# A hybrid retention and SSD block: first loads in smaller pieces, meta-token products padded to 128 rows, the last row block's end in another order

## The chip, the cores and the metric

The kernel runs on one core of a Trainium2 chip. The metric is the device time of one execution in microseconds. The core has a matrix engine (TensorE, PE in the profile; its weight loads are listed as PEld), a vector engine (DVE), a scalar engine (ACT), a general engine (POOL), and the sync engine (SP), which here only issues transfers. ACT issues some transfers too. The engines run side by side and wait for each other through semaphores; each of them does its own instructions in order.

## What is computed

One layer of a hybrid encoder over 512 frames of width 1024, behind 16 learned meta tokens. Cut to what matters:

```
hn = rmsnorm(h) * norm1_w
q, k, v, g, z, xbc, dt = split(hn @ w_in)           # 1024 x 7184
y_ret = GroupNorm(retention(q, k, v)) * silu(g)     # 8 heads of 128
y_ssd = GatedRMSNorm(ssd(silu(conv4(xbc)), dt), z)  # 4 groups of 4 heads of 64
h = h + concat(y_ret, y_ssd) @ w_out                # 2048 x 1024
h = h + relu(rmsnorm(h) @ w_ff1)**2 @ w_ff2         # 1024 x 4096 x 1024
out = rmsnorm(h)[the 512 frames] * final_norm_w
```

Retention and SSD both carry a state from one run of tokens to the next. The meta tokens form a first, short run of 16; its contribution to the first state is a product over 16 tokens for each SSD group and for each retention head. All values are float32. Each large product is done as three: both operands are split into a part that the matrix engine's fast float32 format (fp32r) holds and the rest, and high by high, high by rest and rest by high are summed.

## The kernel before

**Start (lines 128 to 315).** Twenty products of zeros (`warm`, L135) run on PE while the first transfers are under way. The transposed input comes as `xr` in two runs of tokens, 272 and 256, each in two transfers of four of the eight slices of width 128 (L147, on SP's queue, behind `pc`, the column constants with norm1's weights). The first weights `wzr` (the z columns of SSD group 0 and the dt columns) come in two transfers on ACT's queue (L143). Then SP issues the meta tokens, row constants, two of the four row blocks of x, the identity, the two weight transfers of the next projection (`ahead_load(1)`), the other two row blocks, and `cst`. `gain_split` (L273, L274) makes the high part `hnh` of a slice on DVE or ACT and the rest `hnl` on DVE; `split` (L151, L152) does the same for weights, ACT the high part and DVE the rest. `inv_rms` (L280 to L282) takes each row block's sum of squares on ACT and its power on POOL.

**First projection.** `z_first` (L420) multiplies two pairs of 128-token blocks; the second pair needs the second run of tokens. A small product for the meta tokens' dt (`pdm`, L427) needs `hm` (L424) from DVE. Then `conv_silu` runs the B columns of group 0: a product over 272 tokens, then `rms_row` as a hook (L289 to L294: small PE products that turn the row factors into a row `rsr`), then the eviction of the first product with `rsr` (L393), then a product over 256 tokens and its eviction. Four columns of convolution on DVE (L397, L399) follow.

**Weaving.** The SSD cores and the retention cores are generators, advanced by one step each time the projection in front yields, so their small float32 products lie between the projection's. `dt_gen` computes the step sizes on DVE (L338 to L353) and then the cumulative sums on PE (`acs`, L359). The tile framework orders the instructions of each engine by program order and by its own estimate of when they are ready.

**Meta-token products.** In `ssd_core` the first state is a product of `bt[:M, 3, :]` and `xmw`, both 16 rows high (L528), once for each of 4 groups. In `ret_core` it is `mk[:, 0, :]` by `mk[:, 1, :]`, 16 rows high (L685), once for each of 8 heads. A plain float32 product shows as two records on PE.

**End.** `token_gemm` multiplies by w2 for two halves of 512 columns; in each, the last four (or two) k-slices are finished block by block, so that block 3's products end last (L779). `fin_b`, for each of four blocks of 128 rows, adds the product to the residual (DVE, L1026), sums squares (ACT, L1041), forms the factor (POOL, L1042, L1043), scales the second half (DVE, L1044) and the first half (ACT, L1046) and writes them from SP's and ACT's queues (L1045, L1047). `nwb` holds the final norm's weights on all rows (loaded at L1061).

## Time and profile before

| | |
|---|---|
| median of 3 runs | 866.22 us (866.08 to 866.31) |
| the profiled execution | 866.04 us |
| its span, first to last instruction | 864.3 us |
| PE busy | 851.9 us (99%) |
| DVE, ACT, POOL busy | 557.8, 406.6, 30.9 us |
| moved | 84.69 MB, mean 98 GB/s |

In the profile PE's clock is the granted one, as a share of full speed. A row of the timeline gives the start, the duration, the engine, the line, the operation, the written and the read names, the shapes, a count of merged instructions, and, in brackets, how long the engine had been idle before and what ended that.

### The profile page before, as it was taken

Reading aid. Unit: us, or ns where it says so; the run is one execution under the profiler, and the core shown is the slowest. Engines: PE = TensorE matmul, PEld = TensorE weight load, DVE = VectorE, ACT = ScalarE, POOL = GpSimd, SP = SyncE. Lnnn points to the kernel's source line nnn. Section 1 sums busy time; section 2 is a strip of 40 time slices with the busy share of each in tenths; the row PEclk is TensorE's granted clock in tenths of the full one; section 3 lists DMA queues with packets and bytes.
Section 4 is the critical chain, followed back from the end, with each engine's and each line's share of the span. In section 5 each row is a group of like instructions: output and inputs, shape, how many; then the busy total and the mean of one; then the engine's idle time right before and its main releaser. Section 6 shows DMA issues by size and latency. Waiting matters only on the chain.

```text
span 864.3 us, 13343 instructions
## 1 busy us (share of the span) xinstructions
PE 851.9 (99%) x5566; PEld 767.4 (89%) x5566; DVE 557.8 (65%) x872; ACT 406.6 (47%) x683; POOL 30.9 (4%) x58
## 2 busy tenths in 40 slices
PE   8999999999999999999999999999999999999995
PEld 6999999999889988999888889999999888888884
DVE  5799887978745564455455549988887544464432
ACT  6673627272432323232353457577667533443432
POOL 1000010010000000000000000000000000000001
PEclk9999999999999999999999999999999999999999
DMA  8833323333231313122222221333335433332002
GB/s 314 241 124 98 114 85 97 113 84 98 74 98 49 98 50 98 55 93 58 89 84 91 86 66 65 99 98 99 98 99 164 153 98 98 97 98 98 0 1 98
DMA packets 84221, 84.69 MB, mean 98 GB/s; under 512 B 2336, under 2 KB 67104, under 8 KB 84160
## 3 DMA queue, kind: packets, MB, share of 16 engines
q1 hardware_dynamic: 83296, 81.68, 30.7%
q10 hardware_dynamic: 864, 2.16, 0.7%
q8 instruction: 43, 0.70, 0.3%
q14 instruction: 18, 0.15, 0.1%
HBM read 81.70 MB, written 2.13 MB: 97 GB/s over the span
## 4 chain that ended last, share of the span: by engine, by line
PE 91%; DVE 5%; ACT 1%; issue 1%; DMA 1%; POOL 1%; POOLq 0%; SPq 0%; DVEq 0%; ACTq 0%
PE acc L753 10%; PE acc L754 10%; PE acc L752 10%; PE fb L970 8%; PE fd L970 5%; PE pj L324 3%; PE pj L326 3%; PE pj L325 3%; PE fa L970 3%; PE pz L447 3%; PE pk L324 2%; PE pk L326 2%; PE pv L324 2%; PE pv L326 2%; PE pv L325 2%; PE pk L325 2%
## 5 line engine op out<-in xcount | busy, mean ns | idle before, releaser
L151 ACT ACTIVATE wh<-wr 128x1024 fp32r<-128x1024 f32 x146 | 153.8, 1057 | 215.5 <-issue 66.8
L152 DVE TENSOR_TENSOR wh<-wr,wh 128x1024 fp32r<-128x1024 f32 x146 | 178.1, 1222 | 116.9 <-ACT wh L151 116.8
L753 PE MATMUL acc<-wh,mh 128*128 128x512 f32 x370 | 145.7, 394 | 0.4 <-DVE mh L152 0.4
L752 PE MATMUL acc<-wh,mh 128*128 128x512 f32 x370 | 145.9, 396 | 0.0
L754 PE MATMUL acc<-wh,mh 128*128 128x512 f32 x370 | 145.7, 394 | 0.0
L753 PEld LDWEIGHTS acc<-wh,mh 128*128 128x128 f32 x370 | 69.4, 188 | 17.0 <-DVE mh L152 0.9
L754 PEld LDWEIGHTS acc<-wh,mh 128*128 128x128 f32 x370 | 69.4, 188 | 16.4
L752 PEld LDWEIGHTS acc<-wh,mh 128*128 128x128 f32 x370 | 69.3, 188 | 15.8
L324 PE MATMUL pj<-hnh,wh 128*128 128x256 f32 (+2 forms) x256 | 73.7, 288 | 0.0
L326 PE MATMUL pj<-hnh,wh 128*128 128x256 f32 (+2 forms) x256 | 72.8, 285 | 0.0
L325 PE MATMUL pj<-hnl,wh 128*128 128x256 f32 (+2 forms) x256 | 72.8, 284 | 0.0
L970 PE MATMUL fb<-hs,wh 128*128 128x256 f32 x576 | 70.7, 280 | 0.1
L970 PEld LDWEIGHTS fb<-hs,wh 128*128 128x128 f32 x576 | 69.1, 188 | 0.3 <-DVE wh L152 0.3
L325 PEld LDWEIGHTS pj<-hnl,wh 128*128 128x128 f32 x256 | 48.4, 189 | 0.0
L324 PEld LDWEIGHTS pj<-hnh,wh 128*128 128x128 f32 x256 | 48.3, 189 | 0.0
L326 PEld LDWEIGHTS pj<-hnh,wh 128*128 128x128 f32 x256 | 48.2, 188 | 0.0
L970 PE MATMUL fa<-hs,wh 128*128 128x256 f32 x384 | 47.8, 281 | 0.3 <-ACT a_lo L975 0.3
L970 PE MATMUL fd<-hs,wh 128*128 128x256 f32 x384 | 46.7, 280 | 0.0
L970 PEld LDWEIGHTS fa<-hs,wh 128*128 128x128 f32 x384 | 46.1, 189 | 0.4 <-ACT a_lo L975 0.4
L970 PEld LDWEIGHTS fd<-hs,wh 128*128 128x128 f32 x384 | 45.9, 188 | 0.1
L151 ACT ACTIVATE mh<-a_lo 128x512 fp32r<-128x512 f32 x48 | 29.4, 623 | 20.6 <-PE acc L754 18.3
L152 DVE TENSOR_TENSOR mh<-a_lo,mh 128x512 fp32r<-128x512 f32 x48 | 32.5, 687 | 8.9 <-ACT mh L151 8.9
(265 smaller groups left out, 1651.7 us busy)
## 6 DMA issues: line engine op xcount, KB each, us to landing
wr<-in_w_ff_dram SPq DMA_DIRECT2D x30, 1024.0 KB, 5.3
wr<-in_w_in_dram SPq DMA_DIRECT2D x40, 512.0 KB, 5.2
wr<-in_w_out_dram SPq DMA_DIRECT2D x8, 1024.0 KB, 5.0
wr<-in_w_in_dram SPq DMA_DIRECT2D x7, 1024.0 KB, 8.6
lt<-acsd SPq DMA_DIRECT2D x16, 256.0 KB, 3.9
xt<-in_x_dram SPq DMA_DIRECT2D x4, 512.0 KB, 9.0
a_lo<-in_w_ff_dram SPq DMA_DIRECT2D x2, 1024.0 KB, 6.8
wzr<-in_wzd_dram ACTq DMA_DIRECT2D x2, 544.0 KB, 5.4
```

The lines of the kernel that those rows point to most:

```text
L151: ACT.activation(dst_h, src, AF.Copy)
L152: DVE.tensor_tensor(dst_l, src, dst_h.bitcast(F32), op=ALU.subtract)
L324: PE.matmul(ps[:, :n], lhsT=wh[:, k, :], rhs=hnh[:, k, t0:t0 + n], start=(k == 0), stop=False)
L325: PE.matmul(ps[:, :n], lhsT=wh[:, k, :], rhs=hnl[:, k, t0:t0 + n], start=False, stop=False)
L326: PE.matmul(ps[:, :n], lhsT=wl[:, k, :], rhs=hnh[:, k, t0:t0 + n], start=False, stop=(k == KT - 1))
L447: PE.matmul(o, lhsT=a[:, k, tk], rhs=zp[k // 4][y][:, k % 4, :], start=(i == 0), stop=(i == len(seq) - 1))
L752: PE.matmul(acc[b], lhsT=s[:, 0, tk], rhs=wh[:, kk, :], start=(k == 0), stop=False)
L753: PE.matmul(acc[b], lhsT=s[:, 1, tk], rhs=wh[:, kk, :], start=False, stop=False)
L754: PE.matmul(acc[b], lhsT=s[:, 0, tk], rhs=wl[:, kk, :], start=False, stop=(k == nk - 1))
L970: PE.matmul(o, lhsT=w[:, y, k, cs], rhs=h[:, z, k, :], start=(q in (1, 6, 5) and t == 0 and k == 0 and i == 0), stop=(k == 3 and i == 2), ...
```

## The change

Fewer products of zeros run at the start (13 for 20). `pc` moves from SP's queue to the head of ACT's; `wzr` comes in three transfers (slices 0 and 1, 2 and 3, 4 to 7) and the first run of `xr` likewise, the second run still in two; the first weight half is split in two pieces. The two transfers of the next projection's weights go ahead of the meta tokens and x. In the one `conv_silu` with a hook, both products come first, then `rms_row`, then both evictions. The meta-token operands become buffers of 128 rows that POOL fills with zeros once (`btm`, `xmw`, and two `mk`), of which 16 rows are written, and their products take all 128 rows. At the end, block b's sum and squares come ahead of the scaling of block b-1; the last block is summed and scaled in runs of 256 columns; the weights `nwb` are scaled by the square root of 1024 on ACT, so that the mean's division goes. The diff, cut to its core (the layout of `wzd` follows that of `wzr`):

```diff
-NWARM = 20
+NWARM = 13
...
+    btm = sp.tile([P, P], F32, name="btm")
+    xmw = sp.tile([P, 256], F32, name="xmw")
     POOL.memset(ones, 1.0)
...
-    nc.sync.dma_start(out=pc, in_=pcols)
-    for j in range(2):
-        nc.scalar.dma_start(out=wzr[:, j], in_=wzd[:, j])
-    for i, (t0, n) in enumerate(HV):
-        for j in range(2):
-            o = KT * t0 + 4 * j * n
-            nc.sync.dma_start(out=xr[i][:, 4 * j:4 * j + 4, :], in_=xtr[:, o:o + 4 * n].rearrange("p (k n) -> p k n", n=n))
+    nc.scalar.dma_start(out=pc, in_=pcols)
+    for k0, k1 in ((0, 2), (2, 4), (4, 8)):
+        nc.scalar.dma_start(out=wzr[:, k0:k1], in_=wzd[:, k0:k1])
+    for i, k0, k1 in ((0, 0, 2), (0, 2, 4), (0, 4, 8), (1, 0, 4), (1, 4, 8)):
+        t0, n = HV[i]
+        o = KT * t0 + k0 * n
+        nc.sync.dma_start(out=xr[i][:, k0:k1, :], in_=xtr[:, o:o + (k1 - k0) * n].rearrange("p (k n) -> p k n", n=n))
...
-            split(hv, lv, wzr[:, j])
+            for k0, k1 in ((0, 2), (2, 4)) if j == 0 else ((0, 4),):
+                split(hv[:, k0:k1], lv[:, k0:k1], wzr[:, 4 * j + k0:4 * j + k1])
...
+    ahead_load(1)
     nc.sync.dma_start(out=mt, in_=meta)
     nc.sync.dma_start(out=hr, in_=hrows.partition_broadcast(P))
-    for b in range(2):
+    for b in range(NB):
         nc.sync.dma_start(out=xt[b], in_=x[b * P:(b + 1) * P, :])
-    nc.sync.dma_start(out=idt, in_=cident)
-    ahead_load(1)
-    for b in range(2, NB):
-        nc.sync.dma_start(out=xt[b], in_=x[b * P:(b + 1) * P, :])
+        if b == 1:
+            nc.sync.dma_start(out=idt, in_=cident)
     POOL.memset(dtv, 0.0)
+    POOL.memset(btm, 0.0)
+    POOL.memset(xmw, 0.0)
     nc.sync.dma_start(out=cst, in_=cpack)
...
+        def evict(ps, t0, n):
+            DVE.tensor_tensor(pre[:, 3 + t0:3 + t0 + n], ps[:, :n], rsr[:, t0:t0 + n], op=ALU.mult)
+        out = []
         for t0, n in ((t_in, 272 - t_in), (272, 256)):
             ps = psum(pp, "pj")
             mm_cols(ps, n, wh, wl, t0)
-            if hook:
-                hook()
-                hook = None
-            DVE.tensor_tensor(pre[:, 3 + t0:3 + t0 + n], ps[:, :n], rsr[:, t0:t0 + n], op=ALU.mult)
+            out.append((ps, t0, n))
+            if not hook:
+                evict(*out.pop())
+        if hook:
+            hook()
+            for o in out:
+                evict(*o)
...
-        xmw = sw.tile([M, 256], F32, tag="xmw", name="xmw", bufs=1)
-        bt = sw.tile([P, 4, P], F32, tag="bt", name="bt", bufs=1)
+        bt = sw.tile([P, 3, P], F32, tag="bt", name="bt", bufs=1)
...
-        ACT.activation(bt[:M, 3, :], psm[:M, 256:256 + P], AF.Copy)
+        ACT.activation(btm[:M], psm[:M, 256:256 + P], AF.Copy)
...
-        PE.matmul(ps[:, :256], lhsT=bt[:M, 3, :], rhs=xmw, start=True, stop=True)
+        PE.matmul(ps[:, :256], lhsT=btm, rhs=xmw, start=True, stop=True)
...
-        mk = rw.tile([M, 2, P], F32, tag="mk", name="mk")
+        mk = RC["mk"][h % 2]
...
-        DVE.tensor_scalar(mk[:, 0, :], psm[:M, 0:P], cst[:M, K_KDM + h:K_KDM + h + 1], None, op0=ALU.mult)
-        ACT.activation(mk[:, 1, :], psm[:M, P:2 * P], AF.Copy, scale=rsc[:M, 0:1])
+        DVE.tensor_scalar(mk[:M, 0, :], psm[:M, 0:P], cst[:M, K_KDM + h:K_KDM + h + 1], None, op0=ALU.mult)
+        ACT.activation(mk[:M, 1, :], psm[:M, P:2 * P], AF.Copy, scale=rsc[:M, 0:1])
...
+            RC["mk"] = [rp.tile([P, 2, P], F32, name=f"mk{i}") for i in range(2)]
+            for t in RC["mk"]:
+                POOL.memset(t, 0.0)
...
-        add_h2(0)(b, acc)
-        ss = small.tile([P, 1], F32, tag="ss", name="ss")
-        ACT.activation(yo[b][:, H0], xt[b][:, H0], AF.Square, accum_out=ss)
-        POOL.tensor_scalar(ep[b], ss, 1.0 / D, EPS, op0=ALU.mult, op1=ALU.add)
-        DVE.tensor_tensor(yo[b][:, H0], xt[b][:, H0], nwb[:, H0], op=ALU.mult)
+        v = xt[b][:, H0]
+        DVE.scalar_tensor_tensor(v, acc, rs2[b], v, op0=ALU.mult, op1=ALU.add)
+        ACT.activation(yo[b][:, H0], v, AF.Square, accum_out=ep[b])
+        POOL.tensor_scalar(ep[b], ep[b], D * EPS, None, op0=ALU.add)
+        DVE.tensor_tensor(yo[b][:, H0], v, nwb[:, H0], op=ALU.mult)
     def fin_b(b, acc):
-        add_h2(1)(b, acc)
-        ss = small.tile([P, 1], F32, tag="ss", name="ss")
-        rs = small.tile([P, 1], F32, tag="rs", name="rs")
-        ACT.activation(yo[b][:, H1], xt[b][:, H1], AF.Square, accum_out=ss)
-        POOL.tensor_scalar(rs, ss, 1.0 / D, ep[b], op0=ALU.mult, op1=ALU.add)
+        last = b == NB - 1
+        for c in (slice(512, 768), slice(768, 1024)) if last else (H1,):
+            v = xt[b][:, c]
+            DVE.scalar_tensor_tensor(v, acc[:, c.start - 512:c.stop - 512], rs2[b], v, op0=ALU.mult, op1=ALU.add)
+            ss = small.tile([P, 1], F32, tag="ss", name="ss")
+            ACT.activation(yo[b][:, c], v, AF.Square, accum_out=ss)
+            if c.stop < 1024:
+                POOL.tensor_tensor(ep[b], ep[b], ss, op=ALU.add)
+        if b:
+            scale_b(b - 1)
+        rs = rss[b]
+        POOL.tensor_tensor(rs, ss, ep[b], op=ALU.add)
         POOL.tensor_tensor(rs, rs, powc[:, 0:1], op=ALU.pow)
-        DVE.scalar_tensor_tensor(yo[b][:, H1], xt[b][:, H1], rs, nwb[:, H1], op0=ALU.mult, op1=ALU.mult)
-        nc.sync.dma_start(out=out[b * P:(b + 1) * P, H1], in_=yo[b][:, H1])
-        ACT.activation(yo[b][:, H0], yo[b][:, H0], AF.Copy, scale=rs)
-        nc.scalar.dma_start(out=out[b * P:(b + 1) * P, H0], in_=yo[b][:, H0])
+        if last:
+            scale_b(b)
+    def scale_b(b):
+        o = out[b * P:(b + 1) * P, :]
+        w = 256 if b == NB - 1 else 512
+        for c in range(0, 512, w):
+            l, r = slice(c, c + w), slice(512 + c, 512 + c + w)
+            DVE.scalar_tensor_tensor(yo[b][:, r], xt[b][:, r], rss[b], nwb[:, r], op0=ALU.mult, op1=ALU.mult)
+            nc.sync.dma_start(out=o[:, r], in_=yo[b][:, r])
+            ACT.activation(yo[b][:, l], yo[b][:, l], AF.Copy, scale=rss[b])
+            nc.scalar.dma_start(out=o[:, l], in_=yo[b][:, l])
...
+    ACT.activation(nwb, nwb, AF.Copy, scale=float(D) ** 0.5)
```

## Rows read from the trace of the kernel before

**Rows 1.** The page: busy time of each engine, and the chain that ended last.
```profile
PE 851.9 (99%) x5566; PEld 767.4 (89%) x5566; DVE 557.8 (65%) x872; ACT 406.6 (47%) x683; POOL 30.9 (4%) x58
...
PE 91%; DVE 5%; ACT 1%; issue 1%; DMA 1%; POOL 1%; POOLq 0%; SPq 0%; DVEq 0%; ACTq 0%
```
**Rows 2.** Timeline, start: start us, us, engine, line, op, out<-in, count [idle before].
```profile
1.17 7.39 PE L135 MATMUL warm<-wz 128*128 128x512 bf16 x20 [1.17 <-DVE wz L129]
...
7.10 0.96 PEld L135 LDWEIGHTS <-wz 128*128 128x128 bf16 x5 [0.26 <-issue]
7.30 0.63 DVE L273 TENSOR_SCALAR hnh<-xr,pc 128x272 fp32r<-128x272 f32 x2 [6.19 <-DMA xr<-in_xtr_dram]
...
8.97 0.94 ACT L271 ACTIVATE hnh<-xr,pc 128x272 fp32r<-128x272 f32 x2 [3.03 <-DMA xr<-in_xtr_dram]
...
12.06 1.29 DVE L152 TENSOR_TENSOR wz<-wzr,wz 128x1088 fp32r<-128x1088 f32 x1
...
13.27 4.08 DVE L274 SCALAR_TENSOR_TENSOR hnl<-xr,pc,hnh 128x272 fp32r<-128x272 f32 x10
...
17.26 0.29 DVE L424 TENSOR_TENSOR hm<-hnh,hnl 128x128 f32<-128x128 f32 x1
```
**Rows 3.** Transfers, 0 to 30 us: rate in 40 slices; a wait of SP's queue.
```profile
GB/s 0 0 57 167 432 400 441 400 435 406 428 431 404 399 153 36 199 422 408 390 333 322 290 300 327 368 410 396 366 360 349 347 335 303 292 284 291 313 344 352
```
```profile
SPq L299 <- DMA xr<-in_xtr_dram: 1.5, 1, 1.5
```
**Rows 4.** First core: a window (length; busy of PE, PEld, DVE, ...), two timeline rows.
```profile
39.00:42.00 3.00, 3.00 (x27) 3.00 (x27) 3.00 (x9) 0.72 (x1) 0.00 (x0) 1.00 1.14 309
```
```profile
42.80 0.23 DVE L353 SCALAR_TENSOR_TENSOR dt<-tdt,negA 128x80 f32<-128x80 f32 x1
...
43.27 1.05 PE L359 MATMUL acs<-cst,dt 128*16 128x128 f32 x8
```
**Rows 5.** PE's timeline beside an SSD and a retention meta-token product; weight loads (ns).
```profile
57.86 0.28 PE L325 MATMUL pj<-hnl,wh 128*128 128x260 f32 x1
...
60.09 1.05 PE L544 MATMUL cb<-cf,bf 128*128 128x128 f32 x8
...
262.38 0.28 PE L326 MATMUL pk<-hnh,wh 128*128 128x256 f32 x1
...
263.78 1.06 PE L694 MATMUL sc<-qr,kr 128*128 128x128 f32 x8
```
```profile
L685 PEld LDWEIGHTS kv<-mk x16: 181/183/185, 234.4 to 429.0; 16*128 16x128 f32 x16
...
L687 PEld LDWEIGHTS kv<-vt,kd x48: 186/192/193, 234.8 to 429.8; 128*128 128x128 f32 x48
```
**Rows 6.** PE's timeline where full-height float32 products follow a projection.
```profile
242.18 0.28 PE L326 MATMUL pv<-hnh,wh 128*128 128x256 f32 x1
242.29 0.38 PE L701 MATMUL o<-vt,pt 128*128 128x128 f32 x2
242.51 0.39 PE L702 MATMUL o<-s,qr 128*128 128x128 f32 x2
```
**Rows 7.** Timeline, the last 12 us of the span.
```profile
852.57 2.96 PE L779 MATMUL acc<-wh,mh 128*128 128x512 f32 x12
...
856.21 0.75 DVE L1044 SCALAR_TENSOR_TENSOR yo<-xt,rs,nwb 128x512 f32<-128x512 f32 x1 [1.79 <-POOL rs L1043]
856.88 0.75 DVE L1026 SCALAR_TENSOR_TENSOR xt<-acc,rs,xt 128x512 f32<-128x512 f32 x1
...
858.48 0.26 POOL L1042 TENSOR_SCALAR rs<-ss,ep 128x1 f32<-128x1 f32 x1 [2.31 <-ACT yo L1041]
...
859.41 0.72 ACT L1046 ACTIVATE yo<-yo,rs 128x512 f32<-128x512 f32 x1 [1.03 <-POOL rs L1043]
...
860.16 0.37 ACTq L1047 DMA_DIRECT2D out_dram<-yo  x1
```
**Rows 8.** The page's groups: ACT's work on 1024 columns (busy, mean ns, idle before).
```profile
L151 ACT ACTIVATE wh<-wr 128x1024 fp32r<-128x1024 f32 x146 | 153.8, 1057 | 215.5 <-issue 66.8
```

More of the change, by code (lines that the diff above doesn't have):

```diff
@@ L122 @@
     ZN = 256 + SH
-    wzr = dtp.tile([P, 2, 4, ZN], F32, name="wzr")
+    wzr = dtp.tile([P, KT, ZN], F32, name="wzr")
     dtv = dtp.tile([P, NCH, SH], F32, name="dtv")
@@ L426, in z_first @@
                 for k in range(KT):
-                    PE.matmul(pdm, lhsT=hm[:, k, :], rhs=wzr[:, k // 4, k % 4, 256:], start=(k == 0), stop=(k == KT - 1))
+                    PE.matmul(pdm, lhsT=hm[:, k, :], rhs=wzr[:, k, 256:], start=(k == 0), stop=(k == KT - 1))
                 DVE.scalar_tensor_tensor(dtv[:M, 0, :], pdm, rsc[:M, 0:1], dtbias[:M], op0=ALU.mult, op1=ALU.add)
@@ L495, in ssd_core @@
         PE.transpose(psm[:M, 256:256 + P], bf[:, 0:M], ident)
-        DVE.tensor_tensor(xmw.rearrange("p (h e) -> p h e", e=HD), psm[:M, :256].rearrange("p (h e) -> p h e", e=HD),
+        DVE.tensor_tensor(xmw[:M].rearrange("p (h e) -> p h e", e=HD), psm[:M, :256].rearrange("p (h e) -> p h e", e=HD),
                           bc4(tdw[:M, 0, hs], M), op=ALU.mult)
-        ACT.activation(bt[:M, 3, :], psm[:M, 256:256 + P], AF.Copy)
+        ACT.activation(btm[:M], psm[:M, 256:256 + P], AF.Copy)
         ps = psum(pm, "btp")
@@ L501, in ssd_core @@
             PE.transpose(ps[:, c * P:(c + 1) * P], bf[:, M + c * P:M + (c + 1) * P], ident)
-        ACT.activation(bt[:, 0:3, :], ps[:, :3 * P].rearrange("p (c n) -> p c n", n=P), AF.Copy)
+        ACT.activation(bt, ps[:, :3 * P].rearrange("p (c n) -> p c n", n=P), AF.Copy)
         def tb(t, c2):
@@ L1018 @@
     weave(first_products())
-    ys, yo, ep = [], [], []
-    def add_h2(hf):
-        def f(b, acc):
-            v = xt[b][:, hf * 512:(hf + 1) * 512]
-            DVE.scalar_tensor_tensor(v, acc, rs2[b], v, op0=ALU.mult, op1=ALU.add)
-        return f
-    def fin_a(b, acc):
-        add_h2(0)(b, acc)
-        ss = small.tile([P, 1], F32, tag="ss", name="ss")
-        ACT.activation(yo[b][:, H0], xt[b][:, H0], AF.Square, accum_out=ss)
-        POOL.tensor_scalar(ep[b], ss, 1.0 / D, EPS, op0=ALU.mult, op1=ALU.add)
-        DVE.tensor_tensor(yo[b][:, H0], xt[b][:, H0], nwb[:, H0], op=ALU.mult)
@@ L1037, in fin_b @@
-    def fin_b(b, acc):
-        add_h2(1)(b, acc)
-        ss = small.tile([P, 1], F32, tag="ss", name="ss")
-        rs = small.tile([P, 1], F32, tag="rs", name="rs")
-        ACT.activation(yo[b][:, H1], xt[b][:, H1], AF.Square, accum_out=ss)
-        POOL.tensor_scalar(rs, ss, 1.0 / D, ep[b], op0=ALU.mult, op1=ALU.add)
-        POOL.tensor_tensor(rs, rs, powc[:, 0:1], op=ALU.pow)
-        DVE.scalar_tensor_tensor(yo[b][:, H1], xt[b][:, H1], rs, nwb[:, H1], op0=ALU.mult, op1=ALU.mult)
-        nc.sync.dma_start(out=out[b * P:(b + 1) * P, H1], in_=yo[b][:, H1])
-        ACT.activation(yo[b][:, H0], yo[b][:, H0], AF.Copy, scale=rs)
-        nc.scalar.dma_start(out=out[b * P:(b + 1) * P, H0], in_=yo[b][:, H0])
+    yo, ep, rss = [], [], []
@@ L1065 @@
     ep += [ys.tile([P, 1], F32, name=f"ep{b}") for b in range(NB)]
+    rss += [ys.tile([P, 1], F32, name=f"rss{b}") for b in range(NB)]
     weave(second)
@@ L1092 @@
     wf = np.asarray(w_in)[0]
-    wzd = np.concatenate([wf[:, C_Z:C_Z + 256], wf[:, C_DT:C_DT + SH]], axis=1).reshape(2, 4, P, 256 + SH).transpose(2, 0, 1, 3)
+    wzd = np.concatenate([wf[:, C_Z:C_Z + 256], wf[:, C_DT:C_DT + SH]], axis=1).reshape(KT, P, 256 + SH).transpose(1, 0, 2)
     rope, mask, cpack, gpow = _constants()
```

## The prediction

> **What bounds the kernel now.** I read the page first. PE is busy for 851.9 us of a span of 864.3, and 91% of the chain that ended last is PE's own work [rows 1]. So an edit gains only where it shortens PE's stream, fills one of its gaps, or shortens the two ends where PE does no useful work: the start and the stretch behind the last product. The reader should look at four places.
>
> The timeline of the start shows zero products from 1.17 us on (the load that starts the last five is at 7.10, with the fifteenth product), and DVE sits idle for 6.19 us until the first `xr` transfer has landed at 7.30 [rows 2]. From there DVE works without a pause worth naming until `hm` ends at 17.55: 10.25 us of conversions that PE follows. The rate view shows why the transfers come no sooner: 400 to 440 GB/s from 3 to 10.5 us, then three slices of 153, 36 and 199, in a stretch in which SP's queue had been held back by earlier transfers (one such wait is 1.5 us) [rows 3]. The timeline around a 16-row product shows lost time between PE's records although every engine is busy [rows 5], which full-height products do not show [rows 6]. The timeline of the end shows a chain over DVE, ACT and POOL with PE idle [rows 7].
>
> **Padding the meta-token products.** At a retention head, the last projection record starts at 262.38 and the group behind the meta-token product and its three followers at 263.78: 1.40 us [rows 5]. Between them lie one projection record and eight float32 records of 128 columns. At full height such steps take 0.11 us for the projection record and 0.22 for two float32 records, with nothing lost on entry [rows 6]. So the nine should take 0.11 + 8 x 0.11 = 0.99, and 0.41 is lost. At an SSD group, the step from 57.86 to 60.09 is 2.23 [rows 5]; one projection record and eight float32 records of 256 columns, at twice 0.11 each, make 0.12 + 1.76 = 1.88, so 0.35 is lost. Padded to 128 rows the product has the form of its neighbours, and I take the loss as gone: 8 heads x 0.41 + 4 groups x 0.35 = 4.7 us, all of it in PE's stream, which is the bound. The bounds: 4.0 if the step between kinds of product keeps 0.06 each time, 5.0 at best. Other 16-row products (L289, L365, L367) stay as they are.
>
> The weight load itself takes 183 ns at 16 rows and 192 at 128 [rows 5], so the extra rows cost nothing that could be seen; nor do they save anything in the instruction. The Trainium skill, "TensorE: Matmul & The Clock Gate", section on LDWEIGHTS, says that a load of 32 rows takes as long as one of 128; the two medians agree with it. Read alone, that rule says that the row count is no price at all and padding buys nothing, which would take the 4.7 out of the sum; it is a rival below. What speaks for the gain is the spacing of the records, not their duration.
>
> POOL gets four memsets. POOL is busy 4% of the span [rows 1]; the first two lie in its idle start, the `mk` pair waits for memory that the SSD stage gives up, and only the first head's copies wait for it, a projection ahead of their product. Nothing.
>
> **The start.** The first `xr` piece is half as large and no longer behind `pc`. When DVE started at 7.30, some 2.0 MB had moved in all (the slices up to there summed) for 0.6 MB landed on SP's queue [rows 3]. By the same ratio 272 KB land when 0.9 MB have moved, at about 4.8 us: DVE starts 2.5 us earlier. That is the most the start can give. The slices 4 to 7 land no earlier than before by more than `pc`'s share, at about 8.7 for 8.97 [rows 2], since the same bytes are in front of them. By then DVE has the first four slices and the first weight half behind it. What is left for it is 12 rests at 0.41, a weight rest at 1.29 and `hm` at 0.29 [rows 2], 6.5 us, plus about 0.5 until ACT has made the next high part and 0.7 while ACT makes the weight's high part: 8.7 + 7.7 = 16.4 for 17.55. PE follows `hm`, so PE gains 1.15 us. The 13 zero products end at 1.17 + 13 x 0.42 = 6.7, when the first slices are converted (an estimate: 4.8 plus four steps of 0.3 to 0.4).
>
> What is late next: the weights of the next projection now go ahead of x, and the slow slices at 10.5 to 12.8 [rows 3] should fill, so x's last blocks land no later. The second product of the B columns no longer waits behind `rms_row`, but it needs a PSUM buffer that the first z products hold until ACT has scaled them by factors of x; a wait there can take back the 1.15. `rsr` comes after 24 more records of 0.12 us, 2.8 us of PE's stream; both evictions then run back to back on DVE. I take 1.15, bounds 0 and 2.5.
>
> The Trainium skill, "Perfetto Trace Analysis", DMA Optimizations, says that splitting transfers lets work start sooner where the DMA engines are mostly idle, and that large transfers use the bandwidth better. Here they are not idle while the pieces move; by that rule this term would be 0, which the rate row does not bear out alone, since a split changes the order in which bytes land and not only the rate.
>
> **The end.** PE's last record ends at 852.57 + 2.96 = 855.53. Block 3's sum starts at 856.88, behind block 2's scaling, which waited for POOL until 856.21 [rows 7]. With the sum first it can start at 855.55. From the sum's start to the factor took 859.41 - 856.88 = 2.53; in two runs the first square overlaps the second sum, which saves about 0.15 (halves of 0.75 and 0.72 cost some 0.42 each, an estimate). POOL's add for the first run is hidden by the second square. So the factor is there at 857.95, 1.45 us earlier. Then ACT scales a run (0.42), issues (0.37) and scales the next (0.42): the last issue is at 859.3, for 860.16, a gain of 0.85. Block 2's scaling and its issue on ACT, 0.72 + 0.37, now lie between block 3's squares and its scaling and end at about 858.1, at no cost above 0.15. I take 0.8; bounds 0.3 (if DVE still does block 2's scaling first) and 1.4 (if the last issue follows the factor as closely as SP's).
>
> ACT's scaling of `nwb`, 1024 columns, costs about 1.06 us of ACT, which has 215.5 us of idle time ahead of work of this kind [rows 8]. I cost it at nothing; without that cover it delays the splits behind it on ACT, and PE through them, by up to 1.1.
>
> **The sum.** 4.7 + 1.15 + 0.8 = 6.65 us off the profiled execution's 866.04, which lies 0.18 under the median: 866.22 - 6.65 = 859.57, say 859.6.
>
> **The rivals.**
> - The start's lead is lost in the first core, chance 0.15. DVE is busy 3.00 of 3.00 us at 39 to 42, and its last step ends at 43.03, 0.24 ahead of the PE product that needs it [rows 4]. If DVE comes no earlier, PE waits there for all but 0.24 of its lead. For it: that margin, and `rsr`'s later place. Against: PE has projection work to put in front. Time 860.7.
> - The pieces land no earlier because the transfers are saturated, chance 0.07; the term is 0 and the time 860.7 again.
> - Padding buys nothing: the loss hangs on something other than the height, chance 0.07. Against it stand two kinds of product with a like loss. 859.6 + 4.7 = 864.3.
> - ACT reaches `nwb`'s scaling before its load has landed and holds the splits behind it, chance 0.05. ACT's order decides; at 1.1 to 3 us the time is 860.7 to 862.6.
> - Slower: the clock stays at its lower level into the first projection. Zero products of 512 columns started 0.42 us apart until 7.10 (5.93 us for 14 steps), which is the 1.2 GHz level, and five loads later took 0.96 us in all, the 2.4 GHz level [rows 2]; the granted column reads 1.00 later on [rows 4]. Now the zero products end at 6.7, before that rise. If PE then waits and the rise comes late, each product of 272 columns costs 0.113 us more (272/1.2 against 272/2.4). The first projection has 96 of them: from 59 the whole gain is gone, from 75 it is slower by over 0.2%, and with all 96 the time is 870.4. Against: the first slices should be ready by 6.7. Chance 0.04.
>
> **How the numbers follow.** My forecast, all three terms within their bounds, has 0.62. The range holds best cases of 2.5 + 5.0 + 1.4 = 8.9 us (857.3) and, at the other end, 0 + 4.0 + 0.3 less 1.1 for `nwb` (863.0); it leaves out the padding rival and the clock. A measurement of this kernel can tell about 0.2%, 1.7 us, from no change, a line at 864.5. The forecast, the two start rivals and `nwb` lie under it, the padding rival at 864.3 by halves: faster 0.92, same 0.04, slower 0.04.
>
> **What would show it.** Padding: L685's and L528's records as 128 rows high, and 1.0 for 1.40 us across the same nine records. Start: DVE's first conversion near 4.8, `hm` near 16.4, and `acs` without a wait on DVE. End: block 3's sum within 0.1 us of PE's last record, the last issue some 0.8 us nearer to it. The forecast is wrong if the spacing at padded products stays at 1.40, if `acs` waits for DVE, or if products of the first projection are spaced at 0.23 us.

## The result and the profile after

The changed kernel takes 855.26 us (median of 6 runs, 853.98 to 859.48), against 866.15 (866.01 to 866.31) for the kernel before: a ratio of 0.9887, 95% interval 0.9862 to 0.9911. It is faster, as forecast, but by 10.9 us and not by 6.65, and below the range (857.3 to 863.0). One thing is needed to read the times: most of the kernels here, the one before too, run in one of two groups some 4.85 us apart, which by the traces differ in the pace of the FF1 products (the feed-forward's first product, L970). All six runs of the kernel before are in the upper group here, and four of the six of the changed kernel are in the lower one, so the 10.9 us mix the two; below, kernels are compared group with group.

The page of the changed kernel's profiled execution (855.5 us, span 853.7; the rows answer to [rows 1]):

```profile
PE 839.8 (98%) x5559; PEld 764.5 (90%) x5559; DVE 557.0 (65%) x875; ACT 407.1 (48%) x688; POOL 31.0 (4%) x63
...
PE 92%; DVE 3%; ACT 2%; DMA 1%; issue 1%; POOL 0%; ACTq 0%; POOLq 0%; DVEq 0%
```

PE still bounds the kernel; its busy time is 12.1 us less.

**The start came out the other way round.** Its timeline, to be read against [rows 2] (start us, us, engine, line, operation, [idle before]):

```profile
1.17 5.73 PE L137 MATMUL warm<-wz 128*128 128x512 bf16 x13 [1.17 <-DVE wz L131]
...
3.99 0.63 DVE L276 TENSOR_SCALAR hnh<-xr,pc 128x272 fp32r<-128x272 f32 x2 [2.87 <-DMA pc<-in_pcols_dram]
...
5.32 0.66 ACT L153 ACTIVATE wz<-wzr 128x544 fp32r<-128x544 f32 x1 [1.43 <-DMA wzr<-in_wzd_dram]
...
6.34 0.96 PE L432 MATMUL pz<-wz,hnh 128*128 128x272 f32 x2
...
9.49 0.66 ACT L153 ACTIVATE wz<-wzr 128x544 fp32r<-128x544 f32 x1 [3.52 <-DMA wzr<-in_wzd_dram]
...
10.20 0.59 PE L432 MATMUL pz<-wz,hnh 128*128 128x272 f32 x2 [2.16 <-ACT wz L153]
...
12.14 1.11 ACT L153 ACTIVATE wz<-wzr 128x1088 fp32r<-128x1088 f32 x1 [1.17 <-DMA wzr<-in_wzd_dram]
...
13.30 0.82 PE L432 MATMUL pz<-wz,hnh 128*128 128x272 f32 x2 [1.15 <-ACT wz L153]
...
14.49 4.08 DVE L277 SCALAR_TENSOR_TENSOR hnl<-xr,pc,hnh 128x272 fp32r<-128x272 f32 x10
...
18.49 1.22 DVE L154 TENSOR_TENSOR wh<-wr,wh 128x1024 fp32r<-128x1024 f32 x1
...
19.62 0.29 DVE L436 TENSOR_TENSOR hm<-hnh,hnl 128x128 f32<-128x128 f32 x1
```

ACT's two conversions of the same weights in the kernel before:

```profile
4.83 1.11 ACT L151 ACTIVATE wz<-wzr 128x1088 fp32r<-128x1088 f32 x1 [1.91 <-DMA wzr<-in_wzd_dram]
...
9.81 1.10 ACT L151 ACTIVATE wz<-wzr 128x1088 fp32r<-128x1088 f32 x1
```

x is early: DVE converts at 3.99 for 7.30. But the first weights `wzr` now come in three pieces on ACT's queue, and the second and third are late: ACT sits idle 3.52 and 1.17 us for them, and PE 2.16 and 1.15 us for ACT. Before, the two halves landed 4.1 and 6.7 us behind their issues, and ACT did not wait for the second; now the pieces take 4.1, 7.8 and 10.0 us. PE starts its first projection 1.9 us sooner and then has nothing to do. Its clock follows. Windows of the start (length; busy and count of PE, PEld, DVE, ACT, POOL; granted clock; DMA share; GB/s), the last one with the kernel before's below it:

```profile
4.00:8.00 4.00, 4.00 (x15) 2.22 (x13) 3.45 (x9) 0.66 (x1) 0.00 (x0) 1.00 1.03 408
8.00:10.00 2.00, 0.04 (x1) 0.00 (x0) 0.00 (x0) 0.51 (x1) 0.00 (x0) 1.00 1.01 405
10.00:14.00 4.00, 2.65 (x11) 2.33 (x12) 2.27 (x4) 2.83 (x7) 0.00 (x0) 0.56 1.13 316
14.00:17.00 3.00, 3.00 (x15) 3.00 (x15) 3.00 (x8) 3.00 (x9) 0.00 (x0) 0.50 0.85 209
```

```profile
14.00:17.00 3.00, 3.00 (x25) 3.00 (x26) 3.00 (x9) 3.00 (x8) 0.93 (x1) 1.00 1.11 344
```

After two microseconds in which PE ran one record, the granted clock falls to 0.50, its lower level of 1.2 GHz; PE starts 15 records in the three microseconds from 14 where the kernel before starts 25. (In the first window the column reads 1.00, although the zero products start 0.43 us apart there, the step of the lower level; it does not show the level of that stretch.) `hm` ends at 19.9, 2.4 us later than before and not 1.15 earlier. About half of that is a change of order: DVE ends its rests 1.2 us later than before (18.57 for 17.35), and then makes the rest of the next projection's first weights (L154, 1.22 us), which `ahead_load(1)` now brings earlier, ahead of `hm`. The product of the running sums (`acs`) starts at 45.20 for 43.27 [rows 4].

**The padding did what was forecast.** PE's timeline at a retention head, against [rows 5]:

```profile
264.00 0.28 PE L330 MATMUL pk<-hnh,wh 128*128 128x256 f32 x1
264.12 0.38 PE L696 MATMUL kv<-mk 128*128 128x128 f32 x2
264.34 0.83 PE L698 MATMUL kv<-vt,kd 128*128 128x128 f32 x6
265.01 1.06 PE L705 MATMUL sc<-qr,kr 128*128 128x128 f32 x8
```

The nine records take 1.01 us for 1.40. At three of the four SSD groups the step from the last projection record to `cb` is 1.85 to 1.96 us, for 2.23 to 2.34; at the first one the scheduler mixes the records, and the same 16 take 2.65 for 3.05. That is about 0.38 in each of twelve places, 4.6 us.

**The end gained 0.6, and in another way than forecast.** This is the timeline, against [rows 7]:

```profile
842.68 2.91 PE L793 MATMUL acc<-wh,mh 128*128 128x512 f32 x12
...
846.14 0.75 DVE L1069 SCALAR_TENSOR_TENSOR yo<-xt,rss,nwb 128x512 f32<-128x512 f32 x1 [1.69 <-POOL rss L1060]
846.81 0.87 DVE L1051 SCALAR_TENSOR_TENSOR xt<-acc,rs,xt 128x256 f32<-128x256 f32 x2
...
848.37 0.19 POOL L1059 TENSOR_TENSOR rss<-ss,ep 128x1 f32<-128x1 f32 x1 [0.27 <-ACT yo L1053]
848.64 0.55 POOL L1060 TENSOR_TENSOR rss<-rss,powc 128x1 f32<-128x1 f32 x1
849.22 0.91 ACT L1071 ACTIVATE yo<-yo,rss 128x256 f32<-128x256 f32 x2 [1.00 <-POOL rss L1060]
...
849.76 0.84 ACTq L1072 DMA_DIRECT2D out_dram<-yo  x2
```

PE's last record ends at 845.59, and block 3's sum starts only at 846.81, behind block 2's scaling, as before (855.53 and 856.88). The new order of the calls did not become an order on DVE. What is gained comes from the runs of 256: from the sum's start to the last scaling 2.41 us for 2.53, and from there to the end of the span 4.49 for 4.85. From the end of PE's last record to the end of the span (the tail below) it is 8.1 us for 8.7.

**Most of the difference is in products that the change does not touch.** These are the records that PE starts in two windows, the first inside FF1, the second inside the w2 products (length, busy, count; clock; DMA share; GB/s). The kernel before:

```profile
560.00:640.00 80.00, 80.00 (x682) 1.00 0.34 106
700.00:840.00 140.00, 140.00 (x602) 1.00 0.21 68
```

The changed kernel:

```profile
560.00:640.00 80.00, 80.00 (x708) 1.00 0.33 106
700.00:840.00 140.00, 140.00 (x614) 1.00 0.19 61
```

The lines of code and the shapes are the same, the clock is 1.00 in both, and PE is busy throughout. As the mean difference of neighbouring start times, FF1's 256 columns take 113.3 ns for 117.8, and w2's 512 columns 228.9 for 233.3. Over some 1,100 records behind 540 us, and 732 of w2's 768, that is 4.9 and 3.2 us; w_out's products (512 columns, from 420 us) give another 0.8. The busy column reads the same in both; only the distance of the starts shows the difference.

Put together from milestones (the starts of the same products in the two traces): start and padding together -1.0 by the end of the heads (each alone, below: +3.0 and -4.1), w_out -0.8, FF1 -4.9, w2 -3.2, tail -0.6. That is -10.5 us, and the spans differ by 10.6.

### The profile page after: what moved, and what is told of

It reads as the page before. It is cut to its first block, busy times and chain, and to the rows that moved or that the text cites. A ratio compares the mean times of both kernels' runs of the same rounds, so it can differ in the third digit from the quotient of the medians.

```text
span 853.7 us, 13353 instructions
## 1 busy us (share of the span) xinstructions
PE 839.8 (98%) x5559; PEld 764.5 (90%) x5559; DVE 557.0 (65%) x875; ACT 407.1 (48%) x688; POOL 31.0 (4%) x63
## 4 chain that ended last, share of the span: by engine, by line
PE 92%; DVE 3%; ACT 2%; DMA 1%; issue 1%; POOL 0%; ACTq 0%; POOLq 0%; DVEq 0%
PE acc L768 10%; PE acc L767 10%; PE acc L766 9%; PE fb L984 7%; PE fd L984 5%; PE pz L459 4%; PE pj L328 4%; PE pj L330 4%; PE pj L329 4%; PE fa L984 3%; PE pv L328 2%; PE pk L330 2%; PE pv L330 2%; PE pk L328 2%; PE pv L329 2%; PE pk L329 2%
## 5 line engine op out<-in xcount | busy, mean ns | idle before, releaser
L154 DVE TENSOR_TENSOR wh<-wr,wh 128x1024 fp32r<-128x1024 f32 x146 | 178.0, 1221 | 108.4 <-ACT wh L153 108.4
L984 PE MATMUL fb<-hs,wh 128*128 128x256 f32 x576 | 68.4, 277 | 0.1
L984 PEld LDWEIGHTS fb<-hs,wh 128*128 128x128 f32 x576 | 66.9, 188 | 0.3 <-DVE wh L154 0.3
L154 DVE TENSOR_TENSOR mh<-a_lo,mh 128x512 fp32r<-128x512 f32 x48 | 32.5, 689 | 8.0 <-ACT mh L153 8.0
```

Of the source, the lines that this page charges most:

```text
L154: DVE.tensor_tensor(dst_l, src, dst_h.bitcast(F32), op=ALU.subtract)
L984: PE.matmul(o, lhsT=w[:, y, k, cs], rhs=h[:, z, k, :], start=(q in (1, 6, 5) and t == 0 and k == 0 and i == 0), stop=(k == 3 and i == 2), ...
```

## The experiments

**The three parts alone.** Each is the kernel before with the diff's hunks for that part only. The padding (`btm`, `xmw`, `bt`, `mk`):

```diff
-        PE.matmul(ps[:, :256], lhsT=bt[:M, 3, :], rhs=xmw, start=True, stop=True)
+        PE.matmul(ps[:, :256], lhsT=btm, rhs=xmw, start=True, stop=True)
...
-        mk = rw.tile([M, 2, P], F32, tag="mk", name="mk")
+        mk = RC["mk"][h % 2]
```

> The kernel before with the padding alone. Both theories: the same nine records at a meta-token product take 1.01 us for 1.39, so 12 x 0.38 = 4.6 us less in PE's stream. Theory 1 (pace): the other 8 us of the change come from the step between PE's records in the feed-forward part (113 to 118 ns for 256 columns, 227 to 233 for 512), which is set anew after each wait of PE and by no edit; so the time is 861.6 if the steps stay as before, or lower by up to 9 us in lumps of 2 to 5 us if a wait falls differently. Rival (layout): the new buffers of the padding are what makes the feed-forward part faster, then the time is near 852.5 and the steps are 113 and 229 ns in every execution.

Measured: a median of 861.86 us, ratio 0.9951 (0.9927 to 0.9975). Four runs lie at 856.94 to 857.12 and seven at 861.72 to 862.04, for 861.14 to 861.62 and 866.03 to 866.82 of the kernel before on that chip, which is -4.3 in either group. FF1 and w2 keep 117.8 and 233.3 in its profile.

The start (`NWARM`, pieces, `ahead_load`, hook):

```diff
-    nc.sync.dma_start(out=pc, in_=pcols)
+    nc.scalar.dma_start(out=pc, in_=pcols)
...
+    for k0, k1 in ((0, 2), (2, 4), (4, 8)):
+        nc.scalar.dma_start(out=wzr[:, k0:k1], in_=wzd[:, k0:k1])
```

> The kernel before with the start's edits alone (13 zero products, smaller pieces, weights ahead of x, rms_row behind both products). Theory 1 (pace): the first projection ends 2.8 us later than before, so the time is 869 with the steps of before, less by lumps if a wait falls differently. Rival (the start, with its later clock or its other timing, is what makes the feed-forward part faster): 860 with steps of 113 and 229 ns.

Measured: a median of 867.99, ratio 1.0025 (1.0001 to 1.0049); the groups are 862.94 to 864.41 and 867.18 to 869.29. The part that was to bring 1.15 us costs 1 to 3. In its profile (869.29 us) the last head's `kv` product is 3.05 us late.

The end:

```diff
+        if b:
+            scale_b(b - 1)
+        rs = rss[b]
...
-        rs = small.tile([P, 1], F32, tag="rs", name="rs")
```

> The kernel before with the end's edits alone. Both theories: the stretch from PE's last record to the end of the span is 0.6 us shorter than the 9.1 of before. Theory 1 (pace): 865.6 with the steps of before, or lower in lumps. Rival (the scaling of nwb on ACT or the new buffers at the end change the last product): the last product's step is 229 for 233 ns and the time near 862, with the feed-forward's first product as before.

Measured: a median of 861.92, ratio 0.995 (0.9929 to 0.9972); the groups are 856.97 to 857.11 and 861.84 to 862.30, which is -4.2. In its trace the tail is 0.4 us shorter (8.30 for 8.72). The rest is w2 at 228.9 ns, and w_out at 227 from 420 us on, **before any edited instruction has run**, with the instructions of PE in the same order as before. So it is not the work of the edit.

**One product more**, to see whether FF1's pace hangs on PE's phase:

```diff
+            if n == 9:
+                PE.matmul(banks[(bk, g)][:, :128], lhsT=wsp[n][:, 0, 0, 0:P], rhs=HS[q][:, 0, 0, 0:128], start=True, stop=True, skip_group_check=True)
```

> The kernel before with one more product of 128 columns on PE, at the tenth product of the feed-forward part; its result is overwritten. Theory 1 (pace): the added work costs 0.06 us, but the step of the products behind it may change at that place: either 866.2, or 861 if the step goes from 118 to 113 ns for the remaining 1100 or so records. Rival (layout or clock): the step cannot change, 866.3.

Measured: 866.22 to 866.55 in all 11 runs, ratio 1.0023 (1.0004 to 1.0041). Not one is in the lower group, where the kernel before had 17 of 35 on that chip. The same product is tried again, in padding and end together, further down.

**The place in memory.** The end's edits drop one tag from the pool `small`, and with it 128 bytes, so that what is allocated behind it lies 128 bytes lower. Ahead of the last block, this kernel does only that to the one before:

```diff
-        rs = small.tile([P, 1], F32, tag="rs", name="rs")
+        rs = ss
```

> The kernel before, with fin_b's second small tile dropped (the power is taken in place in ss): no instruction is added, removed or reordered ahead of the last block, and every tile that is allocated behind the pool 'small' lies 128 bytes lower, as it does with the end's edits. Theory 'place': TensorE's step between records of the w_out and w2 products (512 columns) follows where the operands lie, so it falls from 232 to 227 and from 233.3 to 228.9 ns, and the two groups of times lie some 3.6 to 4.2 us under those of the kernel before (861.4 and 866.2), near 857.5 and 862.3. Rival 'work': the step follows what the edited end does or the changed program; then 861.4 and 866.2, step 233.3.

Measured: the groups are 857.52 to 857.93 and 862.37 to 862.47, ratio 0.9934 (0.9914 to 0.9955). The windows of its profile:

```profile
560.00:640.00 80.00, 80.00 (x709) 1.00 0.35 106
700.00:840.00 140.00, 140.00 (x614) 1.00 0.18 61
```

w2 has 614 records for 602, at 228.9 ns. The other way round, these are the end's edits with the 128 bytes given back:

```diff
+        else:
+            POOL.memset(small.tile([P, 1], F32, tag="rs", name="rs"), 0.0)
```

> The end's edits alone, with four unused small tiles of the old tag allocated again (one is set to zero once, in the first of the four final blocks, on POOL), so that every tile lies where it lay in the kernel before. Theory 'place': the step goes back to 232 and 233.3 ns and only the tail's 0.6 us is left of the gain: 860.8 and 865.6. Rival 'work': as the end's edits alone, 857.0 and 861.9, step 228.9.

Measured: 10 of 11 runs at 865.56 to 865.99, one at 860.89; ratio 0.9993 (0.998 to 1.0006). Its window:

```profile
700.00:840.00 140.00, 140.00 (x602) 1.00 0.20 68
```

It is back at 602, and all that is left of the end is its tail, 0.5 us. So the place is shown both ways. The shift of 128 bytes costs something too: at 420 us the kernels with it (the end alone, and the dropped tile) are 0.7 us behind the kernel before, and this one 0.16.

**Padding and end without the start:**

> The padding and the end together, without the edits of the start. If the parts add up as they did singly (padding -4.3, end -4.2, from 861.4 and 866.2): 852.9 and 857.7, so 1 to 3 us under the whole change in either group. If the whole change's fast FF1 step came from its start's edits (which shift the time at which the FF1 products begin), this kernel stays mostly in the slower group, near 857.7.

Measured: 852.76 to 852.85 in 4 runs, ratio 0.9846 (0.9833 to 0.9858). The parts add up to within 0.1 us. Against the lower group of the whole change (853.98 to 855.5), the change without its start is some 2 us faster. All four runs are in the lower group, against the expectation's second half. With the one product more:

> Padding and end, with one 128-column product more ahead of the fourth of the FF1 groups' products at n = 9, as in the kernel before plus one product, which was in the slower of the two groups in all its 11 runs. Theory 'restart': FF1's step (113.3 or 117.8 ns per 256 columns) is set by how PE's stream starts again after its last wait near 540 us, and the added product fixes it at 117.8; all runs then lie near 857.6 + 0.2 and none near 852.8, where all four of padding and end lay. Rival 'chance by chip or layout': the added product does nothing to it, and runs lie near 853.0 as those of padding and end do.

Measured: 853.0 to 853.45 four times, 857.85 and 858.14. Here the added product does not fix the pace, so the theory "restart" falls. Why all 11 runs with it in the kernel before were in the upper group is not explained; what selects FF1's pace in an execution stays open.

**Other places.** These are padding and end with an unused tile in `small`, of 64, 256, 512 or 192 bytes (the lines for 64):

```diff
+    spacer = small.tile([P, 16], F32, name="spacer", bufs=1)
+    POOL.memset(spacer, 0.0)
```

> Padding and end, with one unused small tile of 64 bytes ahead, so that everything behind the pool 'small' lies 64 bytes higher: half way between the place of the kernel before (step of w2's products 233.3 ns) and of the whole change (228.9). Theory 'place': the step is a function of the place and takes one of the levels 226.7, 228.9 or 233.3, in all of the w2 products after PE's last wait; total 852.8 + 768 x (step - 228.9), plus 4.85 if FF1 runs at 117.8. Rival: a chance of each execution; then it says nothing of the place. One look can't tell a new level from chance, but 228.9 in every kernel at -128 bytes and 233.3 in every one at 0 so far speak for the place.

> Padding and end with everything behind the pool 'small' at +128 bytes against the kernel before (+256 against padding and end). 'Place' with a period of 256 bytes: w2's step 228.9 again; 'place' with a period of 512: a value of its own, not 228.9; chance: any. FF1's step 113.3 or 117.8 as it falls. Total 852.8 + 768 x (step - 228.9 ns), plus 4.85 with FF1 at 117.8.

> Padding and end at +384 bytes against the kernel before, which is 512 bytes above the place of padding and end. 'Place' with a period of 512 or less: step 228.9 as there, total 852.8 or 857.6. 'Place' without a short period, or with respect to other buffers by distance: another step.

> Padding and end at +64 bytes against the kernel before. 'Place' that wants multiples of 128 bytes: as bad as -64 bytes (w2 near 232.4, FF1 near 118.7). 'Place' with a period of 256: between or unlike both; no value is named for it ahead. Total 852.8 + 768 x (step - 228.9 ns), plus the FF1 part.

Measured, a single run each: 861.55, 852.93, 852.74 and 859.39. These are the windows with 64 bytes, and below them those with 192:

```profile
560.00:640.00 80.00, 80.00 (x677) 1.00 0.31 97
700.00:840.00 140.00, 140.00 (x605) 1.00 0.20 67
```

```profile
560.00:640.00 80.00, 80.00 (x669) 1.00 0.32 100
700.00:840.00 140.00, 140.00 (x620) 1.00 0.20 68
```

With 256 and 512 both windows are those of padding and end (708 or 709, and 614), and w2 differs at 64 and 192, so the period is 256 bytes. 64 bytes give w2 a value that was not among those expected (232.4 ns), and 192 a better one than any kernel had (226.7), while FF1 gets its worst (120.0).

Laid beside the addresses of the compiled programs, the steps of w_out and w2 have one rule. In w2 the moving operand `wh` (`rhs` in the code) shifts with `small`, and the stationary `mh` (`lhsT`) lies at 224 modulo 256 in 732 of the 768 products. In w_out's first products `mh` lies at 32. By the difference of the two places:

| `wh` - `mh`, modulo 256 | w2, 700 to 840 us (mh 224) | w_out, 436 to 458 us (mh 32) | 512 columns, ns: w2; w_out |
|---|---|---|---|
| 0 | 192 bytes (wh 224) | whole change, end (wh 32) | 226.7; 226.9 |
| 64 | whole change, end (wh 32) | 64 bytes (wh 96) | 228.9; 228.9 |
| 128 | 64 bytes (wh 96) | before (wh 160) | 232.4; 232.4 |
| 192 | before (wh 160) | 192 bytes (wh 224) | 233.3; 233.3 |

The two stretches have different buffers for `mh` and agree at all four. w_out's second half agrees too: there both operands lie at one place in either kernel (160 before, 32 in the whole change), and the step is 227 in both. To test it as a rule, `mh` alone was moved to the place of `wh`, in padding and end (192 bytes, shown) and in the kernel before (64 bytes):

```diff
     nwb = fin.tile([P, D], F32, name="nwb")
+    POOL.memset(fin.tile([P, 48], F32, name="spacer"), 0.0)
```

> Padding and end, with one unused tile of 192 bytes in the pool ahead of the one that holds w2's stationary halves (mh), so that these lie at the same place modulo 256 bytes as the moving weights (wh at 32, mh from 224 to 32). Theory 'distance': with both at one place the step is 226.7 ns, as at +64, 2.2 ns under padding and end for 768 products: 1.7 us less, so 851.1 and 855.9. Rival 'place of wh': wh has not moved, the step stays at 228.9 and the times at 852.8 and 857.6.

> The kernel before with one unused tile of 64 bytes in the pool ahead of mh, so that w2's mh lies at the same place modulo 256 bytes as its wh (160), and nothing else changed. Theory 'distance': w2's step falls from 233.3 to 226.7 ns: 768 x 6.6 ns = 5.1 us less, so 856.3 and 861.1 against 861.4 and 866.2. Rival 'place of wh': 233.3 as before, 861.4 and 866.2.

Measured: a median of 851.35 for the first (850.97 to 851.57, 5 runs, ratio 0.9839, 0.9815 to 0.9862), and groups of 856.5 to 856.98 and 861.61 to 862.05 for the second (ratio 0.9934, 0.9914 to 0.9954). The w2 window of the second, and that of the first:

```profile
700.00:840.00 140.00, 140.00 (x619) 1.00 0.20 68
```

```profile
700.00:840.00 140.00, 140.00 (x619) 1.00 0.19 64
```

There are 619 records at two different places of `wh`, 226.7 ns: in these products the distance of the two operands decides. In the second kernel PE is 0.2 us behind the kernel before at 420 us and still at 680, so only w2 changed its pace. The load of the DMA engines does not decide: at 68 GB/s the window holds 602, 619 and 620 records in three kernels. The expected gains (1.7 and 5.1 us, with all 768 products counted) held to 0.3 us in the first and to 0.6 in the second. In the kernel before, one unused tile of 64 bytes brings 4.5 us. Padding, end and the 192 bytes together are the best version of the study: by medians 14.9 us under the kernel before and 3.9 under the whole change; against the kernel before's own lower group, 10.1.

The rule does not carry over whole to the projections. Their products of 512 columns have `hnh` moving and the weights `wh` standing, and pass through all four distances in every trace; in the kernel before their median steps are 230, 233, 232 and 233 ns at 0, 64, 128 and 192. Equal places are the fastest there too, but 64 brings nothing.

**What in the start costs.** These kernels have a single run each, so they are read from milestones and not from totals: by how much the last head's `kv` product starts later than the kernel before's, at 428.86. The first has `pc` back on SP:

> The start's edits alone, with the load of pc back at the head of SP's queue. Theory 'queue share': what held wzr's second and third piece back (landing at 8.4 and 11.1 us by ACT's waits) is that SP's transfers begin 1 to 2 us earlier, with no pc ahead of them, and take more than half of the bytes from 2 to 7 us; with pc in front ACT's queue moves near 400 KB per us again from 3 to 4 us, the second piece lands before 7 us, the third before 9, and the clock does not fall: hm back near 17, total 1.5 to 3 us under the start's edits alone. Rival 'pieces': the smaller pieces themselves share the engines worse; then the pieces land as before this edit, within 0.5 us, and the clock falls again.

Measured: +1.74 us for the +3.05 of the start alone (total 867.96). ACT's rows:

```profile
3.91 0.66 ACT L151 ACTIVATE wz<-wzr 128x544 fp32r<-128x544 f32 x1 [0.51 <-DMA wzr<-in_wzd_dram]
5.37 0.66 ACT L151 ACTIVATE wz<-wzr 128x544 fp32r<-128x544 f32 x1 [0.80 <-DMA wzr<-in_wzd_dram]
9.76 0.94 ACT L272 ACTIVATE hnh<-xr,pc 128x272 fp32r<-128x272 f32 x2 [3.74 <-DMA xr<-in_xtr_dram]
10.61 1.09 ACT L151 ACTIVATE wz<-wzr 128x1088 fp32r<-128x1088 f32 x1
```

The weights land early again, and the clock stays at 1.00; but now x is late, and ACT waits 3.74 us for it. From 4 to 8 us DMA moves 408 to 422 GB/s in all three kernels (before, the whole change, this one): whichever queue goes first, the other pays. "Queue share" was right on the pieces and the clock; of the total, 1.3 us of the loss went, somewhat less than the 1.5 to 3 expected, and 1.74 stayed. Then come two kernels that go on from this one, without the hook's new order, and with the loads' old order:

```diff
-        if hook:
-            hook()
-            for o in out:
-                evict(*o)
...
+            if hook:
+                hook()
+                hook = None
```

> The start's edits with pc at the head of SP's queue, and without the new order in the first core's first projection (there the evictions stand behind the hook's work; here they are back in front of it). The kernel with pc on SP ran 0.6 us late at the running sums and 0.1 early at 83 us, then lost 1.7 us between 83 and 93 us where PE waits for DVE's halves of weights. Theory 'DVE's order': putting the hook's work ahead of the evictions made DVE late there; without it the second loss is gone and the last head's kv product starts within 0.4 us of the kernel before (428.86). Rival 'supply': the loss comes from the weights' and pieces' later arrival; then it stays at +1.5 to +2.

```diff
-    ahead_load(1)
     nc.sync.dma_start(out=mt, in_=meta)
```

> The start's edits with pc at the head of SP's queue, and with the loads behind the pieces in their old order (meta tokens, rows and two token blocks ahead of the second group of weights). Theory 'DVE's order': still +1.5 to +2 us at the last head's kv product. Rival 'supply': the weights issued early put POOL's and ACT's sums of squares late (mt issued at 8.3 instead of 3.3 us, the sums' product at +2.6 us); with the old order the last kv product is within 0.4 us of the kernel before.

Measured: +0.87 and +0.98. Each took about half of what was left, where its theory expected all of it but 0.4, so neither theory holds alone. Without both:

> The start's smaller pieces and shorter warm-up alone (pc at the head of SP's queue, hook and loads in their old order). If the two halves of the loss add (0.87 and 0.76 us of 1.74), the last head's kv product starts within 0.3 us of the kernel before (428.86): the pieces alone buy nothing and cost nothing. If each half hides the same work, it stays at +0.9. If the pieces buy what the prediction put down for the start (1.15 us), it starts 0.8 us earlier or more.

Measured: +2.24 (total 868.45), so the halves don't add. These are windows of the kernel with the loads' old order, and of this one:

```profile
12.00:16.00 4.00, 4.00 (x33) 3.82 (x32) 4.00 (x11) 4.00 (x10) 0.00 (x0) 1.00 0.91 337
```

```profile
12.00:16.00 4.00, 4.00 (x21) 4.00 (x21) 4.00 (x9) 4.00 (x11) 0.00 (x0) 0.57 0.95 346
```

The clock fell in this one, and PE started 21 records for 33. All five forms of the start begin the first projection 1.9 to 2.4 us sooner, in all five PE is then busy for 1.3 to 2.1 of the 4 us from 8 to 12, where it was for 3.2 before, and none comes out ahead. The clock fell in the start alone and in this kernel (+3.05 and +2.24) and not in the other three (+0.87 to +1.74). With one trace of each, its share stays open.

## Why the prediction was right and wrong

*Padding*, 4.7 us: right. 4.3 us were measured alone, with the records' spacing at 1.01 for 1.40 us, as the prediction said it would show; the bounds 4.0 to 5.0 held. The rival that padding buys nothing is out: the load of `mk` takes 188 ns for 183, and the time falls all the same. The Trainium skill, "TensorEngine Tiling (Array Packing)", Key Properties, says that a change of the tiling mode drains TensorE; a 16-row product among full-height ones may be such a change, and 0.38 us lost in each of the twelve places agrees with it, though no run here shows the mode itself.

*Start*, -1.15 us: wrong in sign. The step that failed is "By then DVE has the first four slices and the first weight half behind it". x came even sooner than forecast (3.99 us for 4.8), but at 8.7 half of that weight half had not landed: ACT made its second piece from 9.49 and DVE the rest of it from 10.18. The term followed x's bytes with care and gave none to the weights' pieces, which share the 400 to 440 GB/s of [rows 3] with them. In the kernel before, `pc` at the head of SP's queue had kept x back and let the weights through, as putting it back shows; moved away, x came first, the second piece of the weights landed by 9.49 and the third by 12.14. The start alone measured +1 to +3 us. The rival that pieces land no earlier had the right row (the saturated transfers) and stopped at 0, where a sum that is fixed and an order that is changed can also lose. The rival of the clock had the right price, and the clock fell in another way: it was up from 6.9 us, when the first projection had begun, and fell behind a wait in the middle of it; some twenty records from 10.6 to 17.3 us then start 0.227 us apart for 0.125.

*End*, -0.8: the mechanism failed and the size was nearly right. "With the sum first it can start at 855.55" did not happen: the sum is still 1.2 us behind PE's last record. That case stood as the lower bound, 0.3, and the runs of 256 columns made it 0.6. That the size came near 0.8 is luck. (The forecast's own steps add up to a last issue at 859.16 and not 859.3; its margin of 0.15 covers that.)

`nwb`'s scaling costs nothing that shows: with the place given back, PE is 0.16 us behind the kernel before at 420 us and 0.17 at 850, with the scaling in between, and the end still keeps 0.5 us of its tail.

*The sum*: 866.2 - 4.3 + 2 to 3 - 0.6 would have been 863 to 864. What brought the time to 855 was no term at all: w_out and w2 at some 4 us, and FF1's pace at 4.85 in four of its six runs (853.98 to 855.5, against 859.12 and 859.48). Beside the start, the failed step is the silent one, that products which the diff doesn't touch keep their pace. Group with group the change is worth 6.4 to 6.9 us (855.0 for 861.4, 859.3 for 866.2), close to the forecast's 6.65. That is luck: a start that lost where it was to gain, and 4 us of w_out and w2 that nobody had counted, cancelled in part. The w_out and w2 part is shown to come from 128 bytes of a dropped tag. FF1's pace is not explained: one kernel falls into either group from one execution to the next, the pace settles behind PE's short waits at 531 and 540 us, and an added product there did not fix it in padding and end. That the whole change drew the lower pace more often than the kernel before is not shown to be its doing.

## What to carry to other kernels

Read the distance of the starts of equal products in the stretches that an edit leaves alone, before a time is put down to the edit: a removed 128-byte tile was worth more here than the reordered end that removed it. Where one transfer is made earlier while the DMA engines are full, write down which one becomes later. And read in the trace whether the scheduled order is the one that the code was rewritten for; at the end of this kernel it was not.

## What the runs showed of the hardware that was not expected

- In w_out and w2 the step between float32r products of 512 columns takes four values by the distance of the moving from the stationary operand modulo 256 bytes: 226.7 ns at 0, 228.9 at 64, 232.4 at 128, 233.3 at 192. The projections' products of 512 columns show only the first and not the second (230 and 233). Products of 256 columns in FF1 (moving operand at 224) run the other way: 120.0 with equal places and 118.7 at a distance of 128 (one trace each), and 113.3 or 117.8 at 64 and 192. What makes the places count was not tried. The Trainium skill, "TensorE: Matmul & The Clock Gate", section "Step-by-step: what each phase is for", says that loading the next weights takes nothing from the read of the running product, since each has a port of its own. That the place of the weights alone moves the step by 6.6 ns does not agree with that, if the two reads are the cause; the measurement decides.
- At the same places FF1's pace is one of two, 4.85 us of the total apart, by execution: on four chips the kernel before was in the lower group 17 times of 35, 2 of 17, 7 of 11 and 2 of 17. No kernel was traced in both groups; that the pace is what separates them is read from traces of different kernels, where 113.3 for 117.8 ns over some 1,100 records is 4.9 us.
